# Delta rule of a hybrid block: 64x64 blocks on diagonal array tiles, four token tiles at once

## The chip, the core and the metric

The kernel runs on one core of one Trainium2 chip. Times are device microseconds. The engines are PE (TensorE; its weight loads are shown as PEld), DVE (VectorE), ACT (ScalarE), POOL (GpSimd) and SP (SyncE, which issues the transfers here).

## What is computed

The program is a two-layer model of width 1024 over 512 tokens. Layer 0 is a hybrid mixer: sliding-window attention and a gated delta rule side by side, one output projection over both. Only the delta rule (4 heads of 128, chunks of 64 tokens) is touched. Per chunk and head it computes

```python
    a_mat = jnp.einsum('bhnik,bhnjk->bhnij', k_beta, k) * decay_strict
    t_mat = lax.linalg.triangular_solve(a_mat + eye, eye, left_side=True, lower=True, unit_diagonal=True)
    u = jnp.einsum('bhnij,bhnjv->bhniv', t_mat, v_beta)
    w = jnp.einsum('bhnij,bhnjk->bhnik', t_mat, k_beta * jnp.exp(g)[..., None])
    qk = jnp.einsum('bhnik,bhnjk->bhnij', q, k) * decay_incl
    def step(S, inp):
        v_new = u_c - jnp.einsum('bhck,bhkv->bhcv', w_c, S)
        o_c = jnp.einsum('bhck,bhkv->bhcv', q_c, S) + jnp.einsum('bhij,bhjv->bhiv', qk_c, v_new)
        S = S * jnp.exp(gl_c)[..., None, None] + jnp.einsum('bhck,bhcv->bhkv', kt_c, v_new)
        return S, o_c
```

where decay_incl and decay_strict are exponentials of differences of the running sums g (with and without the diagonal), q_c is q times exp(g), and kt_c is k times exp(g_last - g). The outputs are normalised per head, gated by z and multiplied by the lower half of `hyb_w_out`; the attention's output is multiplied by the upper half.

## The kernel before

The 512 tokens are four tiles `tt` of 128 tokens on the partitions, so one tile holds two chunks of 64. All the work of the delta rule is in `hybrid()`, in three generators that yield between pieces.

`pair(tt)` makes, for two chunks and four heads at once, all that doesn't depend on the state. A tile of 128x512 holds four heads side by side; each head's 128x128 block is block-diagonal, two chunks of 64x64 with zeros between. POOL multiplies the gates with masks; PE transposes k and v (results times gates to `kb`, `kt`, `vb`); three products of 512 columns (L772, L776, L780) give sums of gates, whose exponentials on ACT are `dec`, `decT` and `eg`; four 128x128 products each of k with k and k with q (`pk`) are multiplied into them (L787, L791); L794 multiplies q by `eg`, head by head. Then the triangular inverse T (`tm`) and its transpose U (`um`) are built by doubling over five levels: POOL masks the off-diagonal part (`al`, L811), PE multiplies `al` with `um` (`py`, L814), ACT copies the odd blocks (L815), PE multiplies `tm` with that (`p1`, L819), DVE subtracts it from `um` (L820), and PE transposes `um` (L824) so that ACT can copy the even blocks into `tm`. Last come u (L829) and w (L834).

`chain(tt)` goes through the two chunks of a tile in turn: w times the state S (L857), subtraction from u on DVE (L858), S times its decay (L863), kt times the new values (L866), S summed (L870), q times S and qk times the new values into `po` (L873, L875); at its end the tile is normalised and turned by `to_ot` (L308 in the profile). It is a serial chain over eight chunks.

`attn_out()` (L265 to L267, 256 columns, 16 items of 12 matmuls) and `delta_out()` (`mm3`, L248 to L250, 512 columns) are the two halves of the output projection: ordinary products that serve as filler. `weave` draws from its generators in proportion to the numbers given. So the order of work is: `pair(0)` and `pair(1)` in turn with all 16 items of `attn_out`; `pair(2)` and `pair(3)` in turn with `chain(0)` and `chain(1)`; then the weights of `delta_out` are asked for, and `chain(2)` and `chain(3)` run with `delta_out`. `pair(tt)` and `pair(tt + 2)` share the six buffers of `seta` (or `setb`). PSUM results go by tags: "acc", "tp" and "mm". The program is put in each engine's order by the framework's scheduler, so it isn't exactly the source's order.

Of the kernel before, what the change touches and what calls it, by code (L numbers as in the profile page):

```python
# [18 lines left out]
P = 128  # L19
# [10 lines left out]
def _consts():  # L30
# [69 lines left out]
class Core:  # L100
# [407 lines left out]
    def hybrid(self, after):  # L508
# [219 lines left out]
        gates()  # L728
        self.gemm_b(w_in, 0, KT, 2304, 260, lhs, z_cb(0))
# [10 lines left out]
        m4 = lambda name: bcast(self.c(name)[:, None, :], [P, 4, P])  # L740
        u, qk, kt, egl = {}, {}, {}, {}
# [3 lines left out]
        sets = [[t[:, i] for i in range(6)] for t in (sa, sb)]  # L745
        qks = [t[:, i] for t in (sa, sb) for i in (6, 7)]
        cp = (lambda o, i: nc.scalar.activation(o, i, AF.Copy), nc.vector.tensor_copy)

        def pair(tt):
            dec, kb, tm, um, al, y = sets[tt % 2]  # L750
            gm, gl, bm, eg = al, y, tm, um
            decT, kt_, vb = qks[tt], self.big(name="kt"), self.big(name="vb")
            cs = slice(tt * P, (tt + 1) * P)
            t4 = slice(tt * 4, tt * 4 + 4)
            g_b = bcast(gg[:, t4, None], [P, 4, P])
            nc.gpsimd.tensor_tensor(h4(gm), g_b, m4("sgt"), op=ALU.mult)
            nc.gpsimd.tensor_tensor(h4(gl), g_b, m4("lincl"), op=ALU.mult)
            nc.gpsimd.tensor_tensor(h4(bm), bcast(beta[:, t4, None], [P, 4, P]), m4("sgt"), op=ALU.mult)

            pt = self.ps("tp")  # L760
# [5 lines left out]
            pt = self.ps("tp")  # L766
            for h in range(4):
                nc.tensor.transpose(pt[:, h * P:(h + 1) * P], ys[8 + h][:, cs], ident)
            nc.vector.tensor_tensor(h4(vb), h4(pt), bcast(hb[:, t4, None], [P, 4, P]), op=ALU.mult)
# [5 lines left out]
            pd = self.ps("acc")  # L775
            nc.tensor.matmul(pd, self.c("sgt"), gl, start=True, stop=True)  # L776
            nc.scalar.activation(decT, pd, AF.Exp)
            nc.gpsimd.tensor_tensor(h4(decT), h4(decT), m4("lincl"), op=ALU.mult)
            pd = self.ps("acc")
            nc.tensor.matmul(pd, self.ones, gl, start=True, stop=True)  # L780
            nc.scalar.activation(eg, pd, AF.Exp)
            yield

            pk = self.ps("acc")
            for h in range(4):
                nc.tensor.matmul(h4(pk)[:, h], ys[4 + h][:, cs], ys[4 + h][:, cs], start=True, stop=True)
            nc.vector.tensor_tensor(dec, pk, dec, op=ALU.mult)  # L787
            pk = self.ps("acc")
            for h in range(4):
                nc.tensor.matmul(h4(pk)[:, h], ys[4 + h][:, cs], ys[h][:, cs], start=True, stop=True)  # L790
            nc.vector.tensor_tensor(decT, pk, decT, op=ALU.mult)  # L791
            qk[tt] = h4(decT)
            for h in range(4):
                nc.vector.tensor_tensor(ys[h][:, cs], ys[h][:, cs], h4(eg)[:, h], op=ALU.mult)  # L794
            e = self.wk.tile([P, 4, 2], F32, tag="egl", name="egl", bufs=NT)
            nc.vector.tensor_copy(e, h4(eg)[:, :, 63::64])
            egl[tt] = e


            nc.gpsimd.tensor_tensor(h4(tm), h4(dec), m4("lev0"), op=ALU.mult)  # L800
            nc.vector.tensor_tensor(h4(tm), bcast(ident[:, None, :], [P, 4, P]), h4(tm), op=ALU.subtract)
            pt = self.ps("tp")
            for h in range(4):
                nc.tensor.transpose(pt[:, h * P:(h + 1) * P], h4(tm)[:, h], ident)
            nc.scalar.activation(um, pt, AF.Copy)
            for n in range(1, 6):

                b = 1 << n
                odd, even = (lambda t, o=o: t.rearrange("p (m q) -> p m q", q=2 * b)[:, :, o:o + b] for o in (b, 0))
                yield  # L810
                nc.gpsimd.tensor_tensor(h4(al), h4(dec), m4(f"lev{n}"), op=ALU.mult)  # L811
                py = self.ps("acc")
                for h in range(4):
                    nc.tensor.matmul(h4(py)[:, h], h4(al)[:, h], h4(um)[:, h], start=True, stop=True)  # L814
                nc.scalar.activation(odd(y), odd(py), AF.Copy)  # L815
                yield
                p1 = self.ps("acc")
                for h in range(4):
                    nc.tensor.matmul(h4(p1)[:, h], h4(tm)[:, h], h4(y)[:, h], start=True, stop=True)  # L819
                nc.vector.tensor_tensor(odd(um), odd(um), odd(p1), op=ALU.subtract)  # L820
                if n < 5:
                    pt = self.ps("tp")
                    for h in range(4):
                        nc.tensor.transpose(pt[:, h * P:(h + 1) * P], h4(um)[:, h], ident)  # L824
                    nc.scalar.activation(even(tm), even(pt), AF.Copy)
            yield
            pu = self.ps("acc")
            for h in range(4):
                nc.tensor.matmul(h4(pu)[:, h], h4(um)[:, h], h4(vb)[:, h], start=True, stop=True)  # L829
            nc.scalar.activation(vb, pu, AF.Copy)  # L830
            u[tt] = h4(vb)
            pu = self.ps("acc")
            for h in range(4):
                nc.tensor.matmul(h4(pu)[:, h], h4(kb)[:, h], h4(um)[:, h], start=True, stop=True)  # L834
            for h in range(4):
                cp[h % 2](ys[4 + h][:, cs], h4(pu)[:, h])
            yield

        S = None
        st = [h4(self.tmp("st", tag="pr")) for _ in range(4)]  # L840

        def chain(tt):
            nonlocal S
            po = self.ps("acc")
            hv = [slice(0, 2), slice(2, 4)]
            for s in range(2):
                yield
                r = slice(s * 64, s * 64 + 64)
                rc = slice(tt * P + s * 64, tt * P + s * 64 + 64)
                last = tt == NT - 1 and s == 1  # L850
                vn = u[tt]
                if S is not None:
                    pw = h4(self.ps("acc"))
                    vn = st[2 + s]
                    for i in hv:
                        for h in range(i.start, i.stop):
                            nc.tensor.matmul(pw[r, h], ys[4 + h][:, rc], S[:, h], start=True, stop=True)  # L857
                        nc.vector.tensor_tensor(vn[r, i], u[tt][r, i], pw[r, i], op=ALU.subtract)  # L858
# [17 lines left out]
                if not last:  # L876
                    S = s2
# [667 lines left out]
```

## Time and profile before

| | us |
|---|---|
| median of 3 runs | 2497.7 (2496.49 to 2499.53) |
| profiled execution | 2498.23 |
| its span | 2496.4 |
| PE busy | 2439.7 (98%) |
| DVE busy | 1388.8 (56%) |
| ACT busy | 1099.2 (44%) |
| POOL busy | 199.3 (8%) |

The mean granted clock of TensorE is 0.992 of full. The span is one execution on the chip; 1.8 us lie around it. The busy shares are means over the whole program, of which the delta rule's stage is one part, so the stage is read by itself, from PE's timeline and from windows, which give each engine's busy time in a stretch.

### The profile page before, as it was taken

The page shows a single profiled execution, that of the slowest core. Times are in us where ns is not written, and L with a number is a line of the kernel's source. Part 1 is how long each engine was busy: PE and PEld are TensorE (multiplying, and loading weights), DVE is VectorE, ACT ScalarE, POOL GpSimd, SP SyncE. Part 2 cuts the span into 40 slices and gives each one's busy share as a digit, 9 for nine tenths or more (in the row PEclk, how much of TensorE's full clock was granted, in tenths as well). Part 3 has the DMA queues.
Part 4 walks back from the last instruction along what each step waited for, and adds up shares of the span by engine and source line. Part 5 has one row for each costly group of instructions (what it writes and reads, how often), then busy time and mean ns, then how long its engine had stood idle before and what let it go on. Part 6 is the DMA issues. An engine that isn't in the chain of part 4 may idle for free.

```text
span 2496.4 us, 32329 instructions
## 1 busy us (share of the span) xinstructions
PE 2439.7 (98%) x12590; PEld 2011.4 (81%) x12590; DVE 1388.8 (56%) x2544; ACT 1099.2 (44%) x2128; POOL 199.3 (8%) x290
## 2 busy tenths in 40 slices
PE   8999899999999999999999999999999999999998
PEld 7778778888888888888899788888877767888887
DVE  4665465343457663443464565656567764656464
ACT  4542224223236632332365573534467754534352
POOL 1005420000020020000021010000011111000000
PEclk9999999999999999999999999999999999999999
DMA  5111003222323333323222123232222211322221
GB/s 193 52 53 51 18 1 127 93 93 93 101 77 102 110 102 94 99 95 92 94 85 85 43 80 107 93 101 93 86 77 68 60 60 35 119 90 96 93 93 68
DMA packets 176784, 210.25 MB, mean 84 GB/s; under 512 B 8191, under 2 KB 137975, under 8 KB 176631
## 3 DMA queue, kind: packets, MB, share of 16 engines
q1 hardware_dynamic: 176631, 208.18, 26.0%
q8 instruction: 99, 1.62, 0.3%
q14 instruction: 54, 0.44, 0.1%
HBM read 206.06 MB, written 2.10 MB: 83 GB/s over the span
## 4 chain that ended last, share of the span: by engine, by line
PE 88%; ACT 4%; DVE 4%; issue 2%; POOL 1%; DMA 0%; DVEq 0%; POOLq 0%; ACTq 0%; SPq 0%
PE mm L242 13%; PE mm L244 13%; PE mm L243 12%; PE acc L265 9%; PE acc L267 9%; PE acc L266 9%; PE mm L265 2%; PE mm L267 2%; PE mm L266 2%; PE acc L242 2%; PE acc L243 2%; PE acc L244 2%; PE tp L499 1%; PE acc L1438 1%; PE acc L819 1%
## 5 line engine op out<-in xcount | busy, mean ns | idle before, releaser
L242 PE MATMUL mm<-xh,whi 128*128 128x512 f32 x1424 | 565.2, 397 | 0.2 <-DVE xr L937 0.2
L244 PE MATMUL mm<-xh,wlo 128*128 128x512 f32 x1424 | 561.8, 394 | 0.0
L243 PE MATMUL mm<-xl,whi 128*128 128x512 f32 x1424 | 559.9, 393 | 0.0
L167 DVE TENSOR_TENSOR wlo<-raw,whi 128x1024 fp32r<-128x1024 f32 (+2 forms) x248 | 302.6, 1221 | 377.6 <-ACT whi L166 376.7
L166 ACT ACTIVATE whi<-raw 128x1024 fp32r<-128x1024 f32 (+2 forms) x248 | 258.5, 1044 | 427.9 <-PE acc L267 265.6
L265 PE MATMUL acc<-whi,hh 128*128 128x512 f32 x864 | 340.6, 394 | 0.0
L266 PE MATMUL acc<-wlo,hh 128*128 128x512 f32 x864 | 340.2, 394 | 0.0
L267 PE MATMUL acc<-whi,hl 128*128 128x512 f32 x864 | 340.1, 394 | 0.0
L242 PEld LDWEIGHTS mm<-xh,whi 128*128 128x128 f32 x1424 | 267.6, 188 | 63.5 <-issue 5.3
L244 PEld LDWEIGHTS mm<-xh,wlo 128*128 128x128 f32 x1424 | 267.5, 188 | 62.1 <-issue 0.3
L243 PEld LDWEIGHTS mm<-xl,whi 128*128 128x128 f32 x1424 | 268.1, 188 | 60.4 <-issue 1.5
L189 ACT ACTIVATE whi<-raw,pcol 128x256 fp32r<-128x256 f32 (+2 forms) x592 | 242.6, 473 | 156.1 <-PE acc L267 65.5
L190 DVE SCALAR_TENSOR_TENSOR wlo<-raw,pcol,whi 128x256 fp32r<-128x256 f32 (+1 forms) x592 | 239.6, 452 | 116.1 <-ACT whi L189 115.6
L265 PEld LDWEIGHTS acc<-whi,hh 128*128 128x128 f32 x864 | 162.3, 188 | 38.1
L267 PEld LDWEIGHTS acc<-whi,hl 128*128 128x128 f32 x864 | 162.4, 188 | 37.9
L266 PEld LDWEIGHTS acc<-wlo,hh 128*128 128x128 f32 x864 | 162.3, 188 | 37.9
L1088 DVE SCALAR_TENSOR_TENSOR cy<-mm,pcol,cy 128x511 f32<-128x511 f32 (+1 forms) x160 | 119.6, 748 | 90.8 <-ACT cy L1086 88.8
L265 PE MATMUL mm<-whi,xh 128*128 128x256 f32 (+1 forms) x448 | 131.5, 294 | 4.9 <-DVE xl L167 1.8
L267 PE MATMUL mm<-whi,xl 128*128 128x256 f32 (+1 forms) x448 | 129.4, 289 | 0.1
L266 PE MATMUL mm<-wlo,xh 128*128 128x256 f32 (+1 forms) x448 | 129.4, 289 | 0.0
L242 PE MATMUL acc<-xh,whi 128*128 128x256 f32 (+1 forms) x368 | 100.3, 287 | 4.9 <-ACT xh L166 3.4
L243 PE MATMUL acc<-xl,whi 128*128 128x256 f32 (+1 forms) x368 | 103.2, 285 | 0.1
(442 smaller groups left out, 3474.6 us busy)
## 6 DMA issues: line engine op xcount, KB each, us to landing
raw<-in_mlp_w_dram SPq DMA_DIRECT2D x128, 512.0 KB
raw<-in_w_up_dram SPq DMA_DIRECT2D x88, 512.0 KB
raw<-in_w_down_dram SPq DMA_DIRECT2D x44, 512.0 KB
raw<-in_hyb_w_in_dram SPq DMA_DIRECT2D x18, 512.0 KB
raw<-in_w_qkv_a_dram SPq DMA_DIRECT2D x18, 512.0 KB
raw<-in_rec_w_in_dram SPq DMA_DIRECT2D x16, 512.0 KB
raw<-in_w_kvf_dram SPq DMA_DIRECT2D x16, 512.0 KB
raw<-in_hyb_w_out_dram SPq DMA_DIRECT2D x8, 512.0 KB
```

The costliest lines, as they stand in the source:

```text
L166: nc.scalar.activation(hi, src, AF.Copy)
L167: nc.vector.tensor_tensor(lo, src, hi.bitcast(F32), op=ALU.subtract)
L189: self.nc.scalar.activation(hi[:, sl], raw[:, sl], AF.Copy, scale=g)
L190: self.nc.vector.scalar_tensor_tensor(lo[:, sl], raw[:, sl], g, hi[:, sl].bitcast(F32), op0=ALU.mult, op1=ALU.subtract)
L242: nc.tensor.matmul(o, w[0], x[0], start=start, stop=False)
L243: nc.tensor.matmul(o, w[0], x[1], start=False, stop=False)
L244: nc.tensor.matmul(o, w[1], x[0], start=False, stop=stop)
L265: nc.tensor.matmul(o, xh, h, start=k == 0, stop=False)
L266: nc.tensor.matmul(o, xh, l, start=False, stop=False)
L267: nc.tensor.matmul(o, xl, h, start=False, stop=k == kn - 1)
L499: nc.tensor.transpose(pt[:, k * P:(k + 1) * P], b, self.c("ident"))
L1088: nc.vector.scalar_tensor_tensor(y[:, s:], ps[:, :T - s], w(2 - s), y[:, s:], op0=ALU.mult, op1=ALU.add)
```

## The change

The chunks' 64x64 blocks are no longer kept in 128x128 blocks with zeros: masks and matrices are 64 wide, a tile of 128x256 holds four heads, with chunk 0 on partitions 0 to 63 and chunk 1 on 64 to 127. `blocks()` multiplies them by eight matmuls of 64x64, each chunk on its own quarter on the array's diagonal, writing its own half of the partitions. The level's transpose of `um` is replaced by a third product, `y` with `tm`, whose even blocks DVE subtracts from `tm`; the first transpose is a product with the identity. The gate masks are multiplied by POOL before the z product. All four tiles are prepared in turn, 84 of the 192 matmuls of `attn_out` between them. After that one `chain()` runs nine steps, with heads 0 and 1 one chunk ahead of heads 2 and 3; the rest of `attn_out`, then `delta_out`, are woven into it. The turn of a finished tile (`to_ot`, now L312) is put off by a step. Cut to its core:

```diff
@@ -37,8 +37,12 @@
     cols["sgt"] = (i > j) & ch
+
+    i, j = r[:, None] % 64, np.arange(64)[None, :]
+    cols["ident2"], cols["lincl2"], cols["sgt2"] = i == j, i <= j, i > j
     for n, b in enumerate((1, 2, 4, 8, 16, 32)):
         cols[f"lev{n}"] = ((i // (2 * b)) == (j // (2 * b))) & (i % (2 * b) >= b) & (j % (2 * b) < b)
+    i, j = r[:, None], r[None, :]
@@ -726,6 +730,18 @@
         gates()
+        x4 = lambda t: t.rearrange("p (x h k) -> p x h k", x=2, h=4)
+        m4 = lambda name: bcast(self.c(name)[:, None, :], [P, 4, 64])
+        tus = [self.big(name="tu") for _ in range(NT)]
+        bms = [x4(self.big(name="bm")) for _ in range(2)]
+        for tt in range(NT):
+            t4 = slice(tt * 4, tt * 4 + 4)
+            g_b = bcast(gg[:, t4, None], [P, 4, 64])
+            nc.gpsimd.tensor_tensor(x4(tus[tt])[:, 0], g_b, m4("sgt2"), op=ALU.mult)
+            nc.gpsimd.tensor_tensor(x4(tus[tt])[:, 1], g_b, m4("lincl2"), op=ALU.mult)
+            nc.gpsimd.tensor_tensor(bms[tt // 2][:, tt % 2], bcast(beta[:, t4, None], [P, 4, 64]), m4("sgt2"), op=ALU.mult)
         self.gemm_b(w_in, 0, KT, 2304, 260, lhs, z_cb(0))
@@ -737,153 +753,181 @@
+        half = [slice(0, 64), slice(64, 128)]
-        sets = [[t[:, i] for i in range(6)] for t in (sa, sb)]
-        qks = [t[:, i] for t in (sa, sb) for i in (6, 7)]
+        sets = [[t[:, 4 * i + j] for j in range(4)] for t in (sa, sb) for i in range(2)]
+        def blocks(o, lhs, rhs):
+            for h in range(4):
+                for r in half:
+                    nc.tensor.matmul(o[r, h], lhs[r, h], rhs[r, h], start=True, stop=True)
         def pair(tt):
-            dec, kb, tm, um, al, y = sets[tt % 2]
+            dec, vb, ya, kb = sets[tt]
+            tu = tus[tt]
+            tm, um = (x4(tu)[:, i] for i in range(2))
+            y, al = (x4(ya)[:, i] for i in range(2))
+            A, qk[tt] = (x4(dec)[:, i] for i in range(2))
...
             pd = self.ps("acc")
-            nc.tensor.matmul(pd, self.c("lincl"), gm, start=True, stop=True)
+            nc.tensor.matmul(pd[:, :256], self.c("lincl"), tu[:, :256], start=True, stop=True)
+            nc.tensor.matmul(pd[:, 256:], self.c("sgt"), tu[:, 256:], start=True, stop=True)
             nc.scalar.activation(dec, pd, AF.Exp)
-            nc.gpsimd.tensor_tensor(dec, dec, bm, op=ALU.mult)
...
+            nc.gpsimd.tensor_tensor(A, A, bms[tt // 2][:, tt % 2], op=ALU.mult)
+            nc.gpsimd.tensor_tensor(qk[tt], qk[tt], m4("lincl2"), op=ALU.mult)
+            eg = self.tmp("eg")
+            pe = [self.ps("acc"), self.ps("acc")]
+            for c, r in enumerate(half):
+                nc.tensor.matmul(pe[c][:, :256], self.ones[r], tu[r, 256:], start=True, stop=True)
+            for c in range(2):
+                nc.scalar.activation(eg[:, c * 256:c * 256 + 256], pe[c][:, :256], AF.Exp)
             yield
             pk = self.ps("acc")
+            for i in range(2):
+                for h in range(4):
+                    for c, r in enumerate(half):
+                        cc = slice(tt * P + c * 64, tt * P + c * 64 + 64)
+                        nc.tensor.matmul(x4(pk)[r, i, h], ys[4 + h][:, cc], ys[4 - 4 * i + h][:, cc], start=True, stop=True)
+            nc.vector.tensor_tensor(dec, pk, dec, op=ALU.mult)
...
+            pt = self.ps("acc")
+            id2 = self.c("ident2")
             for h in range(4):
-                nc.tensor.transpose(pt[:, h * P:(h + 1) * P], h4(tm)[:, h], ident)
-            nc.scalar.activation(um, pt, AF.Copy)
+                for r in half:
+                    nc.tensor.matmul(x4(pt)[r, 0, h], tm[r, h], id2[r], start=True, stop=True)
+            nc.scalar.activation(um, x4(pt)[:, 0], AF.Copy)
+            for n in range(1, 6):
...
+                nc.gpsimd.tensor_tensor(al, A, m4(f"lev{n}"), op=ALU.mult)
+                yield
+                py = x4(self.ps("tp"))[:, 0]
+                blocks(py, al, um)
+                nc.scalar.activation(y, py, AF.Copy)
+                yield
+                p1 = x4(self.ps("acc"))
+                blocks(p1[:, 0], tm, y)
+                if n < 5:
+                    blocks(p1[:, 1], y, tm)
+                nc.vector.tensor_tensor(odd(um), odd(um), odd(p1[:, 0]), op=ALU.subtract)
+                if n < 5:
+                    nc.vector.tensor_tensor(even(tm), even(tm), even(p1[:, 1]), op=ALU.subtract)
+            yield
+            pu = h4(self.ps("acc"))
+            blocks(pu, um, u[tt])
+            nc.scalar.activation(u[tt], pu, AF.Copy)
...
+            wT[tt] = x4(ya)
+            pw = [x4(self.ps("acc"))[:, 0] for _ in range(2)]
             for h in range(4):
+                for c, r in enumerate(half):
+                    nc.tensor.matmul(pw[c][:, h], h4(kb)[r, h], um[r, h], start=True, stop=True)
...
+        def chain():
...
+            for n in range(9):
+                act = [(g, n - g) for g in range(2) if 0 <= n - g < 8]
+                old = [(g, c) for g, c in act if c]
...
+                    for i in range(2):
+                        for g, c in old:
+                            tt, r, cc = rows(c)
+                            nc.tensor.matmul(pw[r, i], wT[tt][:, c % 2, 2 * g + i], st[g][(c - 1) % 2][:, i], start=True,
+                                             stop=True)
...
                 yield
+                if ready:
+                    ready.pop()()
+                new = [(g, c) for g, c in act if c < 7]
+                pS = {g: h4(self.ps("mm")) for g, c in new}
+                for i in range(2):
+                    for g, c in new:
+                        tt, r, cc = rows(c)
+                        nc.tensor.matmul(pS[g][:, i], kt[tt][r, 2 * g + i], u[tt][r, 2 * g + i], start=True, stop=True)
...
+                            nc.vector.scalar_tensor_tensor(s2, s1, e, pS[g][:, i], op0=ALU.mult, op1=ALU.add)
...
+                if n >= 2 and n % 2 == 0:
+                    ready.append(tail(n // 2 - 1, po[n // 2 - 1]))
                 yield
...
-        weave((together(pair(0), pair(1)), 14), (attn_out(), 16))
-        weave((together(pair(2), pair(3)), 14), (chain_of(chain(0), chain(1)), 4))
+        out_a = attn_out()
+        pairs = together(*(pair(tt) for tt in range(NT)))
+        weave((itertools.islice(pairs, 4), 4), (itertools.islice(out_a, 5), 5))
+        weave((pairs, 13), (itertools.islice(out_a, 3), 3))
         nxt, done = after()
...
+        work = chain()
+        weave((itertools.islice(work, 10), 10), (out_a, 8))
+        drain(out_a)
         out = delta_out()
-        weave((chain_of(chain(2), chain(3)), 4), (itertools.islice(out, 4), 4))
+        weave((work, 8), (itertools.islice(out, 4), 3))
         drain(out)
```

How the scheduler places it on the engines is shown at three places. First PE in one level. The rows are instructions in order: line, result from operands, tile, count. Before, two token tiles are in turn (`seta` and `setb`), with transposes between:

```order
L814 MATMUL acc<-seta 128x128 x3
L824 MATMUL tp<-cst,setb 128x128 x4
L814 MATMUL acc<-seta 128x128
L814 MATMUL acc<-setb 128x128 x4
L819 MATMUL acc<-seta 128x128 x4
L819 MATMUL acc<-setb 128x128 x3
L824 MATMUL tp<-cst,seta 128x128 x4
L819 MATMUL acc<-setb 128x128
```

In the changed kernel L767 is the matmul of `blocks()`; the numbers tell the buffers of the four tiles apart:

```order
L767 MATMUL tp_2372<-tu_1628,seta_1774 64x64 x8
L767 MATMUL tp_2382<-tu_1629,seta_1774 64x64 x8
L767 MATMUL tp_2392<-tu_1630,setb_1775 64x64 x8
L767 MATMUL tp_2402<-tu_1631,setb_1775 64x64 x8
L767 MATMUL acc_2412<-seta_1774,tu_1628 64x64 x8
L767 MATMUL acc_2412<-tu_1628,seta_1774 64x64 x8
L767 MATMUL acc_2432<-seta_1774,tu_1629 64x64 x8
L767 MATMUL acc_2432<-tu_1629,seta_1774 64x64 x8
```

The transposes are gone, four tiles stand between a tile's first and second product, and each tile has three groups of eight. Second, DVE between the decays and the first level. Before, for tiles 0 and 1 (the same comes again for 2 and 3):

```order
L787 TENSOR_TENSOR seta<-acc,seta 128x512
L794 TENSOR_TENSOR y<-y,seta 128x128 x2
L791 TENSOR_TENSOR seta<-acc,seta 128x512
L794 TENSOR_TENSOR y<-y,seta 128x128 x2
L801 TENSOR_TENSOR seta<-cst,seta 128x512
L787 TENSOR_TENSOR setb<-acc,setb 128x512
L791 TENSOR_TENSOR seta<-acc,seta 128x512
L794 TENSOR_TENSOR y<-y,setb 128x128 x4
L801 TENSOR_TENSOR setb<-cst,setb 128x512
```

In the changed kernel, in one stretch for all four tiles:

```order
L812 TENSOR_TENSOR seta<-acc,seta 128x512
L815 TENSOR_TENSOR y<-y,eg 128x128 x2
L812 TENSOR_TENSOR seta<-acc,seta 128x512
L821 TENSOR_TENSOR tu<-cst,seta 128x256
L815 TENSOR_TENSOR y<-y,eg 128x128 x3
L821 TENSOR_TENSOR tu<-cst,seta 128x256
L812 TENSOR_TENSOR setb<-acc,setb 128x512
L815 TENSOR_TENSOR y<-y,eg 128x128 x4
L821 TENSOR_TENSOR tu<-cst,setb 128x256
L812 TENSOR_TENSOR setb<-acc,setb 128x512
L815 TENSOR_TENSOR y<-y,eg 128x128 x4
```

L812 takes the place of L787 and L791, L815 that of L794, L821 that of L801; the q products of all tiles now stand in the row ahead of the last tiles' L821. Third, PE in the chain. Before, one step over all heads, ending with the next step's first product:

```order
L857 MATMUL acc<-st,y 64x128 x2
L866 MATMUL acc<-st,kt 128x128 x2
L873 MATMUL acc<-st,y 64x128 x4
L875 MATMUL acc<-st,setb 64x128 x2
L866 MATMUL acc<-st,kt 128x128 x2
L875 MATMUL acc<-st,setb 64x128 x2
L857 MATMUL acc<-st,y 64x128 x2
```

In the changed kernel, a stretch in the chain's middle, where kt products (L899) and qk products (L912) come two of one group at a time, and one w product (L880) and one q product (L889) stand alone between the fillers:

```order
L899 MATMUL mm<-seta,kt 128x128 x2
L912 MATMUL acc<-seta 64x128
L899 MATMUL mm<-seta,kt 128x128 x2
L912 MATMUL acc<-seta 64x128 x3
L269 MATMUL mm<-whi,oth 128x256
L880 MATMUL tp<-st,seta 64x128
L889 MATMUL acc<-st,y 64x128
L270 MATMUL mm<-wlo,oth 128x256
```

The other three each of L880 and L889 follow behind filler. So where the source writes the two groups in turn, the order doesn't always keep them so.

## Rows read from the trace of the kernel before

**Rows 1.** the page: busy us, share, instructions; the chain of waits by engine

```profile
PE 2439.7 (98%) x12590; PEld 2011.4 (81%) x12590; DVE 1388.8 (56%) x2544; ACT 1099.2 (44%) x2128; POOL 199.3 (8%) x290
...
PE 88%; ACT 4%; DVE 4%; issue 2%; POOL 1%; DMA 0%; DVEq 0%; POOLq 0%; ACTq 0%; SPq 0%
```

**Rows 2.** windows: us, busy of PE, PEld, DVE, ACT, POOL, clock, DMA

```profile
199.00:264.00 65.00, 62.08 (x487) 57.43 (x486) 33.04 (x56) 18.74 (x38) 35.66 (x29) 0.97 0.13 42
264.00:322.00 58.00, 50.25 (x354) 43.72 (x353) 28.34 (x49) 15.63 (x36) 22.23 (x18) 0.94 0.03 10
322.00:364.00 42.00, 41.80 (x243) 29.51 (x241) 27.49 (x75) 5.96 (x12) 7.33 (x11) 1.00 0.00 1
```

**Rows 3.** PE's timeline in a level: start, us, instruction, records, [idle before <-releaser]

```profile
224.78 1.05 PE L819 MATMUL acc<-seta 128*128 128x128 f32 x8
225.67 0.83 PE L819 MATMUL acc<-setb 128*128 128x128 f32 x6
226.35 0.66 PE L824 MATMUL tp<-cst,seta 128*128 128x128 f32 x4
```

**Rows 4.** PE's timeline where tiles 2 and 3 pass from decays to levels

```profile
277.36 0.63 PE L804 MATMUL tp<-cst,seta 128*128 128x128 f32 x4 [2.39 <-DVE seta L801]
...
282.78 0.66 PE L804 MATMUL tp<-cst,setb 128*128 128x128 f32 x4 [2.83 <-DVE setb L801]
```

**Rows 5.** groups by form: busy, mean ns, idle before; L794: ns least/middle/most

```profile
L811 POOL TENSOR_TENSOR setb<-setb,cst 128x512 f32<-128x512 f32 x10 | 12.9, 1289 | 6.6 <-PE acc L814 6.6
...
L820 DVE TENSOR_TENSOR setb<-setb,acc 128x256 f32<-128x256 f32 x10 | 4.2, 420 | 7.9 <-PE acc L819 7.9
...
L858 DVE TENSOR_TENSOR st<-vb,acc 64x256 f32<-64x256 f32 x14 | 5.8, 416 | 8.6 <-PE acc L857 8.6
...
L787 DVE TENSOR_TENSOR setb<-acc,setb 128x512 f32<-128x512 f32 x2 | 1.4, 676 | 0.0
...
L794 DVE TENSOR_TENSOR y<-y,setb x8: 276/1058/1367, 218.1 to 281.8; 128x128 f32<-128x128 f32 x8
```

**Rows 6.** PE's timeline at two decay products of `pair(2)`

```profile
265.21 1.02 PE L772 MATMUL acc<-seta,cst 128*128 128x512 f32 x2
266.07 1.02 PE L776 MATMUL acc<-seta,cst 128*128 128x512 f32 x2
```

**Rows 7.** PE's timeline of a later block's attention: tiles sharing the array

```profile
1344.56 0.71 PE L1239 MATMUL acc<-qkT 64*128 64x128 f32 x8
1345.20 0.39 PE L265 MATMUL mm<-whi,xh 128*128 128x256 f32 x1
...
1904.18 1.08 PE L1438 MATMUL acc<-pT,v 128*64 128x512 f32 x4
```

**Rows 8.** PE's timeline of the attention again: 64 moving columns

```profile
1406.37 1.89 PE L1268 MATMUL acc<-v,pT 128*128 128x64 f32 x16
1408.10 0.61 PE L499 MATMUL tp<-cst,pr 128*128 128x128 f32 x4
```

**Rows 9.** PE's timeline in `chain(3)`

```profile
354.60 0.65 PE L857 MATMUL acc<-st,y 128*64 128x128 f32 x4
355.18 0.71 PE L866 MATMUL acc<-st,kt 64*128 64x128 f32 x4
355.81 1.09 PE L873 MATMUL acc<-st,y 128*64 128x128 f32 x8
```

**Rows 10.** windows of PE alone: us, busy, clock, DMA share, GB/s

```profile
174.00:181.00 7.00, 7.00 (x30) 0.51 0.22 75
283.00:290.00 7.00, 6.17 (x31) 0.53 0.01 2
```

**Rows 11.** PE's timeline at the stage's end

```profile
364.76 0.39 PE L248 MATMUL mm<-whi,oth 128*128 128x512 f32 x1
364.99 0.40 PE L249 MATMUL mm<-wlo,oth 128*128 128x512 f32 x1
...
377.39 0.73 PE L242 MATMUL acc<-xh,whi 128*128 128x256 f32 x4
```

More of the change, by code (lines that the diff above doesn't have):

```diff
@@ L793, in pair @@
[L793 to L802, printed above, removed]
@@ new lines, in pair @@
+            for h in range(4):
+                v = ys[h][:, cs].rearrange("p (c k) -> p c k", c=2)
+                nc.vector.tensor_tensor(v, v, x4(eg)[:, :, h], op=ALU.mult)
+            egl[tt] = self.wk.tile([P, 2, 4], F32, tag="egl", name="egl", bufs=NT)
+            nc.vector.tensor_copy(egl[tt], x4(eg)[:, :, :, 63])
+            nc.gpsimd.tensor_tensor(al, A, m4("lev0"), op=ALU.mult)
+            nc.vector.tensor_tensor(tm, m4("ident2"), al, op=ALU.subtract)
+            yield
+            pt = self.ps("acc")
@@ L810, in pair @@
                 yield
[L811 to L815, printed above, removed]
+                py = x4(self.ps("tp"))[:, 0]
+                blocks(py, al, um)
+                nc.scalar.activation(y, py, AF.Copy)
                 yield
-                p1 = self.ps("acc")
@@ L833, in pair @@
[L833 to L836, printed above, removed]
-            yield
[L839 to L846, printed above, removed]
-                yield
[L848 to L858, printed above, removed]
-                if not last:
-                    pS = h4(self.ps("acc"))
-                    s2 = st[s]
-                    if S is not None:
-                        nc.vector.tensor_tensor(s2, S, bcast(egl[tt][:, :, s:s + 1], [P, 4, P]), op=ALU.mult)
-                    for i in hv:
-                        for h in range(i.start, i.stop):
-                            nc.tensor.matmul(pS[:, h], kt[tt][r, h], vn[r, h], start=True, stop=True)
-                        if S is None:
-                            nc.vector.tensor_copy(s2[:, i], pS[:, i])
-                        else:
-                            nc.vector.tensor_tensor(s2[:, i], s2[:, i], pS[:, i], op=ALU.add)
-                if S is not None:
-                    for h in range(4):
-                        nc.tensor.matmul(h4(po)[r, h], ys[h][:, rc], S[:, h], start=h == 0, stop=False)
-                for h in range(4):
-                    nc.tensor.matmul(h4(po)[r, h], qk[tt][r, h, r], vn[r, h], start=S is None and h == 0, stop=h == 3)
-                if not last:
-                    S = s2
@@ L885, in chain, with turn @@
             nc.vector.tensor_tensor(h4(o), h4(o), bcast(ms[:, :, None], [P, 4, P]), op=ALU.mult)
-            oT[tt, 1] = self.to_ot(o)
+            def turn():
+                oT[tt, 1] = self.to_ot(o)
+            return turn
         def together(*gens):
```

86 lines of the change are left out of this document (44 added, 42 removed).

## Prediction

> **What bounds the kernel now.** I read the page's share of engines and chain of waits first: PE is busy 98% of the span and 88% of the chain of waits lies on it [rows 1]. So a microsecond is won by giving PE less to do, or by losing an idle PE, and lost by making PE wait. Next, the windows of the stage. It starts at 199 us and ends where PE takes up the next block's products, L242 at 377.4 [rows 2, 11]: 178 us. PE is busy 62.1 of the first 65 us, 50.3 of the next 58 and 41.8 of 42, while DVE has 28 to 33 and ACT and POOL less [rows 2]. PE is the bound, except that in the second window 8 us of it are idle: there the 16 items of `attn_out` are used up, `chain(0)` and `chain(1)` are the only filler, and PE waits 2.39 and 2.83 us for DVE's L801 in `pair(2)` and `pair(3)` [rows 4]. After such a wait the granted clock is near half, 0.53 of full from 283 to 290 us; but it was also 0.51 from 174 to 181 us with PE never idle [rows 10].
>
> **Prices.** All fp32 products are two records per matmul. Eight records with 128 columns on the full array took 224.78 to 225.67, 0.111 us each, 0.223 a matmul; four transposes 0.11 each [rows 3]. A decay product with 512 columns took 0.86, from 265.21 to 266.07 [rows 6]. Two matmuls on two row tiles (64 rows each) that write two banks overlap: L1239's eight records took 0.64 instead of 0.89; so do column tiles that write one bank, L1438's four records of 512 columns in 1.08 instead of 1.72 [rows 7]. A record with 64 moving columns but 128x128 weights took 1.73/16 = 0.108, no less than one of 128 columns [rows 8]. In the chain, half-array groups took 0.58 and 0.63 for four records, 0.145 to 0.16 each [rows 9].
>
> **The change, part by part.** I put the stage together anew and compare it with 178 us.
>
> *A, transposes and decays of all four tiles.* PE: 36 matmuls of `attn_out` at 0.12, 4.3; 32 transposes, 3.5; eight decay products of 256 columns at 0.43, 3.4 (before: three of 512, 2.6 us, per tile); the two-bank products of `ones` about 1.7. With small gaps 13.6 us. The masks' POOL work (12 operations of 128x256, by half of the 1.29 us of L811's 128x512 [rows 5] 0.65 each) is issued ahead of the z product, under PE work: nothing, and if it were late, at most a few of these.
>
> *B, the change-over from decays to levels.* DVE now has for four tiles at once, in one stretch, four `dec` products (L812), 16 products q\*eg, four `tm` (L821) and `egl`; by the order nothing of the levels can start before `tm`. The q\*eg product (L794 before) took 276 ns at the least and 1058 in the middle of eight, where POOL was working [rows 5]; I take 16 x 0.28 = 4.5, 5 of waiting for POOL, 4 x 0.68 = 2.7 for `dec` by L787's row, and, as an estimate from the same rows, 2.3 for `tm` and `egl`: 14.5 us (10 with no wait for POOL, 18 if half of the products are as slow as the middle one). PE has only 3.5 of packed products (L811 after) and 24 attention matmuls of 2.8 to fill it; it idles 5 to 6 us and loses clock after it. Before, the same work cost idle time once (the 5 us of [rows 4]) and was filled once.
>
> *C, the block products.* Per level and tile, before: 4 + 4 matmuls of 128x128 and 4 transposes, 2.2 us of PE; 20 levels, 43 us with the last level's missing transposes. After: 8 + 8 + 8 matmuls of 64x64 (8 fewer in the last level), 448 in all, and 32 for the first transpose `pt`. One 64x64 matmul should cost half of what 128 columns cost, and share the array with the one on the other diagonal half: 0.223/2/2 = 0.056, taken as **0.06**; I choose this over the 0.108 a record of [rows 8] because there the weights have 128 columns and here 64. 480 x 0.06 = 28.8. `pu` 32 x 0.11 = 3.5, `pw` 3.4, 24 attention matmuls 2.8, six changes of array shape at 0.2 (the 0.14 to 0.19 that four records took over 0.44 in [rows 9]) 1.2, slow clock after B 2. The levels' waits: four tiles are in turn, so between a tile's `py` and its `p1` three other tiles' products of 0.5 us each stand, and between `p1` and the next `py` three of 1.0; ACT's copy, DVE's two subtractions (0.42 for the larger one before) and POOL's 0.65 [rows 5] fit behind them. If that cover were gone, a level would wait some 1.5 us, 7 in all; I take 0. Sum 41.7. Before, with two tiles in turn, L820's ten calls there had 7.9 us of idle DVE ahead of them, waiting for PE [rows 5]: PE was the late one.
>
> *D, the chain.* 116 matmuls, 232 records; at the chain's own 0.145 [rows 9] 33.6 if none overlap. Two groups of heads a chunk apart put partners on opposite halves (L880, L889, L912) or on opposite row tiles in two banks (L899), but the compiled order breaks about half of the pairs (one L880 and one L889 go ahead alone, L899 comes as two of one group, then L912): a quarter saved, 25.2. To it come 108 attention matmuls x 0.118 = 12.7, 34 delta matmuls of 512 columns x 0.23 = 7.9 [rows 11], three turns of four transposes 1.3, and waits. Before, L858's subtraction had 8.6 us of idle time ahead of it over 14 calls [rows 5]; now 9 steps each wait for a subtraction, and a state update, with 12 filler matmuls between; I take 0.75 a step, 6.8. The attention weights now come in two parts, with the delta weights between them: PE waits some 3 us for two tiles' splits, inside the 6.8. Sum 54.
>
> *E, the tail.* After the last chain product 62 of the 96 delta matmuls are left, where before 42 were: 12.6 us from 364.8 to 377.4, of which 42 x 0.23 = 9.7 is the products [rows 11]. So 62 x 0.23 = 14.3, the 2.9 of turns and waits again, and 1 for a shorter cover of the last normalisation: 18.2.
>
> A to E: 13.6 + 14.5 + 41.7 + 54 + 18.2 = 142. Against 178 that is **36 us less**. The profiled execution took 2498.2, 0.5 above the median of the runs shown; 2498.2 - 36 = **2462** (by the median 0.5 less, not told apart). The full-clock sum of PE's work goes the same way: a tile's `pair` before is 8 transposes 0.9, decays 2.6, eight `pk` 1.8, levels 11.1, `u` and `w` 1.8, 18.2 us, 73 for four; after it is 3.5 + 3.4 + 1.7 in A, 3.5 in B and 35.7 in C, 48. With the chain's 33.6 to 25.2 that is 33; so what idle time goes with [rows 4] comes back in B.
>
> The unknown terms, from both sides. Block matmul: 0.056 (nothing added) to 0.216 (two records of 0.108 and no overlap [rows 8]). Chain: all paired 17 and waits of 2, 13 less; none paired and 10 of waits, 12 more. B: 10 to 18. The forecast with these, without the far end of the block price, is 2448 to 2476.
>
> **Rivals.**
> 1. *The halves don't overlap, so it doesn't do what it says.* `blocks()` writes both row tiles' results into one bank. Rows show overlap for row tiles with two banks, and for column tiles in one [rows 7]; a diagonal pair with one bank is neither. If they go one after the other, each of 480 costs 0.12 instead of 0.06: +28.8, `pu` the same +3.5, `qk` +2: 2496, within 0.2% of before. The Trainium skill, "TensorEngine Tiling (Array Packing)", section "Gotcha 1: PSUM Pressure", says that different row tiles write to different banks and can't access one bank at a time; no run here shows that yet, and by it this case, not the forecast, would hold. For it: the only row tiles seen to overlap have two banks. Against: L1438's column tiles share one bank in different partitions, as the diagonal halves do [rows 7]. 12%.
> 2. *Slower: small matmuls cost as much as large ones.* If a record of 64x64 costs what L1268's costs, 0.108, and the halves don't overlap, 480 x (0.216 - 0.06) = +75, and `pu` +3.5: 2462 + 78 = 2540. It decides from 0.06 + 36/480 = 0.135 us a block matmul. For it: 64 columns took as long as 128 [rows 8]. Against: that row's weights have twice the columns. 8%. With overlap, at 0.108, +23: 2485, faster still; 7%.
> 3. *Clock.* At 174 to 181 us, before the stage, the granted clock was 0.51, the 1.2 GHz level, with PE busy throughout [rows 10]; it could be so in C as well. At half clock the 36 us of PE work there double: 2498, no change. 6%.
>
> **Chances.** Forecast 67% (2448 to 2476); 2485 7%; rival 1 12%, rival 2 8%, rival 3 6%. About 0.2%, 5 us, is what can be told from no change. Faster: the forecast, the 2485 case and a quarter of rivals 1 and 3, where only part of the loss comes: 0.78. Same, the rest of these two but 0.02: 0.12. Slower: rival 2 and that 0.02, 0.10. The range goes from 2446 to rival 1's end, 2497; left out are rival 2, part of rival 3 and the forecast's own lower edge, some 17%.
>
> **What would show it.** Block price: L767's groups of eight in PE's timeline, 0.48 us apart if 0.06, 0.96 by rival 1, 1.73 by rival 2. Clock: the windows of the levels, 0.95 or more, or 0.5. B: one stretch of 14 us with PE half idle, its waits named for DVE's L812 and L821. D: L899 and L880 at 0.11 a pair where they stand as pairs; waits for L885 and L904 near 0.7. The stage's last product (L242 before) should start near 341 us. I am wrong if the stage is not shorter by 20 to 50 us, or if time moves outside it.

## The result and the profile after

The changed kernel takes 2462.84 us (median of four, 2462.57 to 2465.93) against 2498.02 for the kernel before, a ratio of 0.986 (95% interval 0.985 to 0.988). 2462 was predicted. The profiled execution took 2465.93 us, its span is 2464.1. The runs below stand on several chips, where the kernel before had medians of 2496.73 to 2498.02; each ratio is to the kernel before on the same chip. One of the four executions of e5_attn_first, 9153.95 us at a mean clock of 0.504, is left out. Windows of the stage in the profile of the changed kernel, cut at the predicted steps A to E (columns as in [rows 2]):

```profile
199.00:214.30 15.30, 15.30 (x101) 11.59 (x99) 11.46 (x21) 5.72 (x12) 11.56 (x14) 1.00 0.23 70
214.30:229.20 14.90, 11.92 (x285) 11.15 (x285) 12.10 (x28) 4.26 (x11) 9.36 (x12) 1.00 0.01 3
229.20:265.50 36.30, 35.81 (x990) 34.74 (x985) 11.04 (x41) 10.19 (x25) 10.13 (x15) 1.00 0.06 18
265.50:319.80 54.30, 50.75 (x388) 40.15 (x386) 35.96 (x98) 8.96 (x14) 4.95 (x9) 1.00 0.10 30
319.80:343.00 23.20, 20.34 (x106) 16.36 (x106) 18.91 (x33) 11.46 (x16) 12.30 (x12) 1.00 0.15 46
```

The clock column holds 1.00 throughout; before it was 0.97 and 0.94 in the first two windows [rows 2]. PE's timeline at three places: the wait in B with the first blocks behind it; one level; the stage's end:

```profile
224.14 0.68 PE L827 MATMUL acc<-cst,tu 64*64 64x64 f32 x16 [1.55 <-DVE tu L821]
224.62 0.51 PE L767 MATMUL tp<-tu,seta 64*64 64x64 f32 x10
226.57 0.68 PE L827 MATMUL acc<-cst,tu 64*64 64x64 f32 x16 [1.43 <-DVE tu L821]
...
229.64 0.63 PE L767 MATMUL acc<-tu,seta 64*64 64x64 f32 x16
230.11 0.63 PE L767 MATMUL acc<-seta,tu 64*64 64x64 f32 x16
230.57 0.63 PE L767 MATMUL acc<-tu,seta 64*64 64x64 f32 x16
...
339.06 0.75 PE L246 MATMUL acc<-xh,whi 128*128 128x256 f32 x4
```

A group of eight block matmuls (16 records) starts 0.47 us after the one before it: 0.058 us a matmul, against 0.223 for the 128x128 ones of [rows 3]. The next block's first product starts at 339.06, where it was 377.39 [rows 11]: 38.3 us sooner, 37.8 of it by the stage itself. The span shrank by 32.3 only. Behind the stage both kernels run the same instructions in the same order; aligned one by one, the lead is 37 to 38 us until 1376, and 33 after 1388. There, in windows of PE alone and in two rows of its timeline, whose lines are L1268 and L499 of before [rows 8]:

```profile
1367.50:1374.50 7.00, 7.00 (x54) 1.00 0.23 75
1374.50:1378.50 4.00, 3.25 (x26) 0.94 0.41 132
1378.50:1387.60 9.10, 9.10 (x43) 0.50 0.00 1
...
1377.62 3.17 PE L1317 MATMUL acc<-v,pT 128*128 128x64 f32 x16
1380.58 1.70 PE L503 MATMUL tp<-cst,pr 128*128 128x128 f32 x7
```

PE is busy all of those 9.1 us, at the 1.2 GHz level, after 4 us in which it was busy for 3.25. L1317's sixteen records take 2.96 us from start to start, where 1.73 is the time in [rows 8], L503's seven 0.22 each, double the 0.11 of a 128-column record in [rows 3], and 4 us are given back. In the first profile of before none of it is there.

### The profile page after: what moved, and what is told of

Read it like the earlier page. It is cut to its first block, busy times and chain, and to the rows that moved or that the text cites. A ratio compares the mean times of both kernels' runs of the same rounds, so it can differ in the third digit from the quotient of the medians.

```text
span 2464.1 us, 33730 instructions
## 1 busy us (share of the span) xinstructions
PE 2410.0 (98%) x13286; PEld 1986.4 (81%) x13286; DVE 1376.0 (56%) x2560; ACT 1090.5 (44%) x2108; POOL 176.7 (7%) x290
## 4 chain that ended last, share of the span: by engine, by line
PE 89%; DVE 4%; ACT 4%; issue 1%; POOL 1%; DMA 0%; DVEq 0%; POOLq 0%; SPq 0%; ACTq 0%
PE mm L246 13%; PE mm L248 13%; PE mm L247 13%; PE acc L269 10%; PE acc L270 10%; PE acc L271 10%; PE mm L269 2%; PE mm L270 2%; PE mm L271 2%; PE acc L246 2%; PE acc L247 2%; PE acc L248 2%; PE tp L503 1%; PE acc L767 1%; PE acc L1487 1%
```

## The experiments

To compare stages I take the time from its first transposes (L762 before, L780 after, each behind twelve attention matmuls) to the next block's first product, and take off the clock's loss: the length of a half-clock stretch times the part of the clock that was missing there. In the first profile of before that is 4.5 x 0.38 + 7.5 x 0.46, from the last two windows of PE alone here; the others are worked out in the same way. The first two rows are the stage's start and its whole window before, the next two the same after:

```profile
200.80 0.60 PE L762 MATMUL tp<-cst,y 128*128 128x128 f32 x4
...
200.80:377.39 176.59, 165.47 (x1129) 0.97 0.07 22
...
200.26 1.04 PE L780 MATMUL tp<-cst,y 128*128 128x128 f32 x8
...
200.26:339.06 138.80, 130.00 (x1825) 1.00 0.09 28
...
218.00:222.50 4.50, 4.04 (x25) 0.62 0.00 0
283.00:290.50 7.50, 6.67 (x34) 0.54 0.01 2
```

| kernel | median us | stage | clock's loss | stage less loss |
|---|---|---|---|---|
| before, first profile | 2498.02 | 176.6 | 5.2 | 171.4 |
| before_again | one time, 2497.21 | 177.4 | 6.9 | 170.5 |
| after, first profile | 2462.84 | 138.8 | 0 | 138.8 |
| after_again | 2464.50 | 141.3 | 3.4 | 137.9 |
| e1_serial | 2473.87 | 147.9 | 1.7 | 146.2 |
| e2_same_chunk | 2469.11 | 144.4 | 1.7 | 142.7 |
| e3_turn | 2468.66 | 143.0 | 1.7 | 141.3 |
| e4_two_tiles | 2475.70 | 146.7 | 3.4 | 143.3 |
| e5_attn_first | 2466.8 (of three) | 146.1 | 8.5 | 137.6 |
| e6_q_later | 2464.20 | 137.4 | 0 | 137.4 |
| e7_triple | 2524.10 | 197.8 | 1.7 | 196.1 |
| e8_lev0_dve | 2461.75 | 136.1 | 0 | 136.1 |
| e9_turn_later | 2458.39 | 138.1 | 3.4 | 134.7 |

**Do the two quarters work at once?** First the order of the halves:

```diff
-            for h in range(4):
-                for r in half:
+            for r in half:
+                for h in range(4):
```

> The order of the eight matmuls of blocks() is turned: first the four heads of chunk 0, then the four of chunk 1; nothing else changes. Theory: the price of 0.058 us a block matmul comes from the two diagonal quarters working at the same time, and they do so only when they are issued in turn. Then a group of eight that takes 0.47 us takes 0.8 to 0.93, the levels and pu (448 and 32 matmuls, the latter 128 columns) grow by 25 to 29 us, minus what waits they had: 2486 to 2492 us in all. Rival: the price is that of one 64x64 matmul by itself (its weights are half as wide), and the quarters don't work together: groups stay at 0.47 us, 2462 to 2466 us.

2473.87 us, ratio to before 0.990 (0.989 to 0.992); the stage is some 8 us longer. Neither end: groups take 0.58 us. PE's timeline shows why, in one group and the start of the next:

```profile
234.19 0.56 PE L767 MATMUL acc<-seta,tu 64*64 64x64 f32 x10
234.54 0.27 PE L767 MATMUL acc<-tu,seta 64*64 64x64 f32 x1
234.59 0.22 PE L767 MATMUL acc<-seta,tu 64*64 64x64 f32 x1
234.65 0.22 PE L767 MATMUL acc<-tu,seta 64*64 64x64 f32 x1
234.65 0.22 PE L767 MATMUL acc<-seta,tu 64*64 64x64 f32 x1
...
234.77 0.56 PE L767 MATMUL acc<-tu,seta 64*64 64x64 f32 x10
```

The next group's chunk-0 matmuls start between the last chunk-1 ones of this group, two records in the same hundredth of a microsecond. So PE pairs work from neighbouring runs by itself, and the edit did not make it serial. The price of one quarter needed another run:

```diff
-                for r in half:
+                for r in (half[0], half[0], half[0], half[1]):
```

> Each chunk-0 product of blocks() is issued three times in a row, then the chunk-1 product once: 16 matmuls in place of 8, in 60 groups, with the same result. It prices one quarter of the array. Theory: a quarter by itself needs 0.117 us a matmul, and 0.058 was two quarters side by side: a group takes 1.40 us instead of 0.47, 56 us more in all. Rival 1: PE takes one 64x64 matmul each 0.058 us, whichever quarter: 0.93 a group, 28 us more. Rival 2, from the run with chunk 0 ahead of chunk 1: a quarter needs 0.088: 1.05 a group, 35 us more.

2524.10 us (two executions; ratio 1.010, 1.008 to 1.012), the stage 57 to 58 us longer. A group of 16 matmuls starts 1.40 us after the one before it:

```profile
236.43 1.56 PE L767 MATMUL acc<-setb,tu 64*64 64x64 f32 x32
237.83 1.56 PE L767 MATMUL acc<-tu,setb 64*64 64x64 f32 x32
239.23 1.56 PE L767 MATMUL acc<-setb,tu 64*64 64x64 f32 x32
```

1.40 / 12 = 0.117 us for each chunk-0 matmul; the chunk-1 ones lie beside them, each record within 0.01 us of the start of a chunk-0 one. The theory's numbers (1.40, 56 us) hold and both rivals' fall. Work that went through one quarter only would add 480 x 0.058 = 28 us to C.

**The staggered heads.**

```diff
-                act = [(g, n - g) for g in range(2) if 0 <= n - g < 8]
+                act = [(g, n) for g in range(2) if n < 8]
```

> The two groups of heads go through the same chunk in the same step (eight steps instead of nine), so that neighbours no longer lie on opposite halves of the array. Theory: staggering saves a quarter of the chain's 33 us of products; without it the stretch of chain() grows by 6 to 10 us, less one step's waits: 2466 to 2472 us, with 0.145 us a record for the w and q products as before. Rival: the chain is paced by its waits and fillers, the overlap saves nothing that counts, and a step less wins 1 to 3 us: 2459 to 2463 us.

2469.11 us (ratio 0.988, 0.987 to 0.990), the stage 4 to 5 us longer. From its start to the next start on PE, idle time left out, a record of the w products takes 0.121 us instead of 0.079, of the q products 0.133 instead of 0.119, of the qk products 0.135 instead of 0.102, of the kt products 0.154 instead of 0.144. So the overlap is real but smaller than hoped, since the order breaks pairs.

**The second product for T.**

```diff
-                if n < 5:
-                    blocks(p1[:, 1], y, tm)
                 nc.vector.tensor_tensor(odd(um), odd(um), odd(p1[:, 0]), op=ALU.subtract)
                 if n < 5:
-                    nc.vector.tensor_tensor(even(tm), even(tm), even(p1[:, 1]), op=ALU.subtract)
+                    pt = x4(self.ps("acc"))
+                    for h in range(4):
+                        for r in half:
+                            nc.tensor.matmul(pt[r, 0, h], um[r, h], id2[r], start=True, stop=True)
+                    nc.scalar.activation(even(tm), even(pt[:, 0]), AF.Copy)
```

> T is got by turning U again (eight 64x64 products with the identity, copied by ACT) instead of by the product y with T that DVE subtracts: as many block matmuls, but these now wait for DVE's subtraction of the same tile. Theory: with four tiles in turn the wait is covered by the other tiles' products, and the second product by itself is worth 0 to 3 us: 2462 to 2467 us. Rival: the shorter loop is what makes the levels run without waits; undone, PE waits 0.5 to 1 us per tile and level, 16 times: 2471 to 2480 us.

2468.66 us (ratio 0.988, 0.987 to 0.990), the stage 2.5 to 3.4 us longer: by the stage the theory's upper end, and PE has no named wait in the levels. In the median it is 4 to 6 us above the changed kernel, between theory and rival. At one mean clock, 0.992, its three executions (2468.37 to 2470.11) are 2 to 4 us above the two of the changed kernel there (2465.93 and 2466.50), so the rest of the median is clock, and I take the stage's number.

**Four tiles or two.**

```diff
-        weave((itertools.islice(pairs, 4), 4), (itertools.islice(out_a, 5), 5))
-        weave((pairs, 13), (itertools.islice(out_a, 3), 3))
+        weave((together(pair(0), pair(1)), 17), (itertools.islice(out_a, 4), 4))
+        weave((together(pair(2), pair(3)), 17), (itertools.islice(out_a, 4), 4))
```

> Tiles 0 and 1 are prepared first, then 2 and 3, as in the kernel before, with four items of the attention's output product in each half. Theory: four in turn is what hides the loop from one product through ACT or DVE to the next; with two, a level's PE work is 2.8 us against a loop of about 2.9, so PE waits 0.3 to 0.8 us a level, ten levels, and the change-over from decays comes twice, each with fewer fillers: 8 to 15 us more, 2470 to 2478 us. Rival: PE's products are enough even with two tiles, and four at once only gathers DVE's work into one stretch: 2460 to 2465 us.

2475.70 us (ratio 0.992, 0.990 to 0.993), in the expected range, but only some 5 us of the 11 to 13 lie in the stage less its clock, and the waits there are hardly more: PE waits 3.6 us for L821 instead of 3.0, and 0.2 for ACT. The levels don't starve with two tiles. The rest is in the main clock: the mean granted clock is 0.990 in all four executions, where the changed kernel's first four had 0.992 once and 0.994 three times, and 0.002 to 0.004 of 2470 us is 5 to 10 us. Why it is lower here stays open.

**The attention's product before the chain.**

```diff
-        weave((pairs, 13), (itertools.islice(out_a, 3), 3))
+        weave((pairs, 13), (itertools.islice(out_a, 11), 11))
```

> All 16 items of the attention's output product run before the chain, beside the pairs; the chain has only the delta product as filler. Theory: the chain's steps need filler, since a step's way from the w product through DVE and the kt product to the new state is longer than its products; without it PE waits 1 us a step in the first five or six, and gets back up to 3 us in the change-over from decays to levels: 2465 to 2472 us. Rival: the chain's products of two groups fill the waits by themselves, and the 3 us are won: 2459 to 2462 us.

2464.4, 2466.8 and 2472.6 us, a ratio of 0.988 (0.986 to 0.990). PE now waits in the chain (0.63, 1.40, 0.49 and 0.51 us ahead of kt products, for L885), but only 3 us in all, and there is a stretch of 18 us at clock 0.53 from 292 to 310 us. Less that loss the stage is as short as the changed kernel's. Where the filler stands decides less than expected; the time's rise is clock, and whether these waits called it forth is not settled.

**What the change left: DVE in B.** The q\*eg products behind the levels:

```diff
-            for h in range(4):
-                v = ys[h][:, cs].rearrange("p (c k) -> p c k", c=2)
-                nc.vector.tensor_tensor(v, v, x4(eg)[:, :, h], op=ALU.mult)
...
                 if n < 5:
                     nc.vector.tensor_tensor(even(tm), even(tm), even(p1[:, 1]), op=ALU.subtract)
+                    v = ys[n - 1][:, cs].rearrange("p (c k) -> p c k", c=2)
+                    nc.vector.tensor_tensor(v, v, x4(eg)[:, :, n - 1], op=ALU.mult)
```

> The 16 products q*eg are written behind the first four levels' subtractions instead of between dec and tm; in DVE's order 9 of them now come behind the last tm. Theory: DVE is what PE waits for in the change-over (2.98 us before L827): the wait goes down to below 1 us, but the nine products, 0.39 us each, then stand ahead of the first level's subtractions, which costs 0 to 1.5 us again: 2460 to 2463 us. Rival: POOL, by its al products, is the late one: the wait stays near 3 us, 2463 to 2466 us.

2464.20 us, no change that can be told (ratio 0.986, 0.985 to 0.988); the stage is 0.5 to 1.4 us shorter, PE's wait for `tm` 1.59 instead of 2.98, not below 1 as the theory had it. DVE's timeline there, then POOL's:

```profile
221.34 0.95 DVE L818 TENSOR_TENSOR tu<-cst,seta 128x256 f32<-128x256 f32 x1
...
223.83 0.93 DVE L818 TENSOR_TENSOR tu<-cst,setb 128x256 f32<-128x256 f32 x1 [0.33 <-POOL setb L817]
...
221.23 0.78 POOL L830 TENSOR_TENSOR seta<-seta,cst 128x256 f32<-128x256 f32 x1
...
223.07 1.41 POOL L817 TENSOR_TENSOR setb<-setb,cst 128x256 f32<-128x256 f32 x2
```

The same subtraction takes 0.41 to 0.43 us in the changed kernel (L821) and 0.93 to 0.96 in three of four calls here, which start while a POOL operation runs and end 0.28 us after it. Work beside POOL is not enough for that: the first call here, at 220.25, took 0.43 although a POOL operation (L817) ran from 220.31 to 221.28; it had started before it. L812, which reads PSUM, took 0.68 beside POOL (from 222.82, with L830 and L817 at work from 222.38 on) as without. So the first masked product went to DVE as well:

```diff
-            nc.gpsimd.tensor_tensor(al, A, m4("lev0"), op=ALU.mult)
+            nc.vector.tensor_tensor(al, A, m4("lev0"), op=ALU.mult)
```

> As the run with the q*eg products behind the levels, and in addition DVE itself makes the first masked product (al by lev0) instead of POOL. Theory: in that run tm (L818) took 0.93 to 0.96 us where POOL was at work and 0.43 where it wasn't, and waited 0.33 for POOL; with POOL out of this stretch tm takes 0.42, al on DVE 0.42, and PE's wait of 1.59 us goes to 0.5 or less; the twelve q*eg products behind it delay the first level by at most 1 us: the stage, less its loss of clock, 136 to 137.5 us, 2460 to 2463 us in all. Rival: DVE's work is the limit, not POOL's: al adds four times 0.4 us and the stage gets longer, 138 to 140 us.

2461.75 us (ratio 0.986, 0.984 to 0.987), the stage 136.1: PE waits 0.38 us for `tm`, as the theory had it, and three of the four subtractions take 0.41. Last, the turn half a step later:

```diff
-                if ready:
-                    ready.pop()()
                 new = [(g, c) for g, c in act if c < 7]
...
+                if ready:
+                    ready.pop()()
                 if n >= 2 and n % 2 == 0:
```

> As the run before it, and the turn of a finished tile (L312) is issued half a step later, behind the kt products. Theory: PE waited 2.5 us in all for the normalised tile (DVE L926) ahead of L312; behind the kt products 1.6 of it is covered, the last tile's 0.9 is not: 1 to 1.6 us less than the run before it, the stage less its loss of clock 134.5 to 136.5 us, 2458.5 to 2462 us in all. Rival: the delta product's first matmuls come later by it and leave the chain without filler: no gain, or 1 us more.

**2458.39 us** (2457.77 to 2459.39; ratio 0.984, 0.983 to 0.986): all four executions lie below all eight of the changed kernel (2461.51 to 2466.50, after_again's among them). Those ran on other chips, and the intervals of the two ratios overlap; but at one mean clock, 0.994, it took 2457.9 to 2459.4 us and the changed kernel 2461.5 to 2463.6. Against the run before it, 1.4 of the median's 3.4 us lie in the stage; that run's own execution at 0.995 took 2457.38. And it is not for the reason given. PE's timeline has the wait still:

```profile
284.64 0.66 PE L312 MATMUL tp<-cst,ob 128*128 128x128 f32 x4
...
286.64 0.32 PE L879 MATMUL tp<-st,setb 128*64 128x128 f32 x1
286.65 0.32 PE L879 MATMUL tp<-st,seta 128*64 128x128 f32 x1
...
293.88 0.63 PE L312 MATMUL tp<-cst,ob 128*128 128x128 f32 x4 [1.65 <-DVE ob L925]
```

The scheduler put the second tile's L312 (293.88) ahead of the kt products again; only the first tile's (284.64) moved behind them. What went away with that is one lone w and q product: at 286.64 all eight stand in pairs, where the run before it, like the changed kernel, has one of each ahead by itself (in the changed kernel at 289.40 us, after a wait of 0.24). PE's next wait for the state, 0.70 us in both, is gone too, but a half-clock stretch lies there now. These are the differences in the chain; the stage less clock is 1.4 us shorter.

**The clock, twice more.**

> The changed kernel once more, unaltered, beside the next three on the same chip. In its first profile PE's clock fell to 0.50 from 1378 to 1388 us, in code that the change doesn't touch, which gave back 4 of the 38 us that the stage had won; the profile of the kernel before has no such stretch. Theory: it belongs to the changed kernel (four altered forms of it had it too): it is there again, and the time is 2462 to 2466 us. Rival: it comes and goes from one execution to the next; then it can be missing here and the profiled time is 2461 to 2463 us.

> The kernel before, unaltered, for a second profile. In its first profile the stage from 199 to 377 us held two stretches at half clock, which cost 5.1 us by the windows (time times the part of the clock that was missing), and none lay in the unchanged code near 1400 us. Theory: where the clock falls changes from one execution to the next, so the stage's length less that loss is what stays: 172 to 174 us, whatever the stretches are here. Rival: the stretches belong to the kernel's own waits and stand at the same places again, 218 to 222 and 283 to 290 us.

The stretch near 1380 us is gone from the second profile of the changed kernel; another has come in the chain. Windows of PE alone, first of after_again, then of before_again:

```profile
300.00:308.00 8.00, 8.00 (x35) 0.57 0.23 67
...
220.00:224.50 4.50, 3.66 (x19) 0.62 0.19 53
278.00:289.00 11.00, 8.49 (x39) 0.53 0.00 0
```

So for the changed kernel the rival holds, it comes and goes (its profiled time, 2463.59, lies just above the rival's range). But it comes more often than it goes: of the eleven profiles of the changed kernel and its altered forms, eight have some 10 us at clock 0.50 at this place of the code and none of the two of before. The three without it (after_again, e5_attn_first, e9_turn_later) have a stretch at half clock in the chain instead; e4_two_tiles has both. What decides it stays open. In the kernel before the two stretches come again, within 5 us of the first profile's, beside the same waits of PE for L801 (2.35 and 2.66 us at 215.37 and 220.84, 2.38 and 0.85 at 277.62 and 281.98, in before_again): there the rival is right, and the stage less its loss is 170.5, below the theory's range. As far as two profiles show, these two belong to the kernel.

## Why the prediction was right

**The price of a block matmul** carried it: 0.058 us against 0.06, by the overlap that was assumed. Rival 1 falls, since a quarter by itself costs 0.117 and two at a time cost what one does, in one bank. The Trainium skill, "TensorEngine Tiling (Array Packing)", section "Gotcha 1: PSUM Pressure", says that different row tiles can't access one PSUM bank at the same time. These rows don't agree for the two diagonal quarters, which write different partitions of one bank, and they decide. Rival 2 falls with it: a 64-column record cost 0.108 us in [rows 8], but 0.058 in one quarter by itself (e7_triple), and L811's 128 records took 3.88 us, 0.030 each. Rival 3 did not occur in C.

**Step by step,** predicted and measured: A ends at 213, 214.3. B 14.5, 14.9; the q\*eg products took 6.1 in DVE's timeline where 9.5 with POOL's waits had been taken, but PE's idle time was 3.0 and not 5 to 6; the first blocks of tiles 0 and 1 (L827 at 221.44, L767 at 224.62 us) started before the last `tm` (226.01), where the forecast had let nothing of the levels start. C 41.7, 36.3: the block price and `pu` (3.5) and `pw` (3.7) as said, no waits in the levels, but 4 us of its first products had been done in B, and the 2 us of slow clock did not come. D 54, 54.3, by terms that err against each other: chain products 25.7 (25.2), attention 14.7 (12.7, since each change of array shape is paid by a filler), delta 9.0 (7.9), waits 3.4 (6.8). The waits were not those that the forecast counted in each step: none is for a subtraction (L885); 1.65 is for a normalised tile ahead of its turn (L926), 0.9 for the state (L907), 0.8 for the attention's second weights. E 18.2, 19.3. From 199 us on that is 140 us against the predicted 142.

**What was not in the sum:** of the 38 us in the first profile 5 were clock, which the kernel before lost behind its waits for L801 and the changed kernel did not lose there (170.5 to 171.4 against 137.9 to 138.8 without clock, 33 us). And 4 us went again in unchanged code, so the profiled execution shrank by 32.3. The three executions that set the median had a mean clock of 0.994, the profiled one 0.992, and were 3 us quicker; no trace shows which stretch they lacked. Without that the median would lie 3 us above the forecast. The full-clock sum of PE's work had 33 us and no change of idle time; between the first profiles PE's busy time in the stage fell from 165.5 to 130.0 us, 31 of it without the clock's part (PE was busy for 8.9 us at half clock there), and its idle time from 11.1 to 8.8. The idle part was misread: [rows 4] have 5 us of waits for L801, but PE's timeline of before has two more, for tiles 0 and 1:

```profile
217.14 0.63 PE L804 MATMUL tp<-cst,seta 128*128 128x128 f32 x4 [2.34 <-DVE seta L801]
...
221.55 0.84 PE L804 MATMUL tp<-cst,setb 128*128 128x128 f32 x4 [0.47 <-DVE setb L801]
```

That is 8.0 us in all, and 3.0 came back in B. The sum was right in kind, and its last 2 to 3 us by luck.

**What each part is worth,** by the stage less clock: overlap of the quarters 28 (worked out from e7_triple's price), of which 8 are lost by a mere change of order; staggering 4 to 5; the second product 3; four tiles in turn 5. They overlap and don't add up to 33.

## What to carry to other kernels

Price a small matmul by the quarter of the array that it uses, and issue neighbours for opposite quarters in turn; then read the compiled order, since the scheduler may part what the source pairs. When a shorter chain leaves a stretch bound by DVE, look at what POOL does in the same moment before moving work to it. Compare stages, not spans, when half-clock stretches come and go that cost 2 to 9 us here, and subtract them openly.

## What was not expected of the hardware

- Runs of four matmuls for one quarter and then four for the other still overlap at their seams: 0.58 us a group, where 0.47 is full overlap and 8 x 0.117 = 0.93 none.
- A DVE subtraction of 128x256 took 0.93 to 0.96 us when it started while a POOL operation ran, 0.43 when it started just before one, and 0.41 with POOL idle.
- The clock stood at 0.50 for 9.1 us with PE busy throughout, in one profile of the changed kernel and not in the other; eight of eleven profiles of it and its altered forms have the stretch.
